# Normalising attention heads in two PSUM steps, with all engines ordered over two periods

## The chip, the cores and the metric

The kernel runs on one core of one Trainium2 chip. The metric is the device time of one launch in microseconds (us), the median of several runs of the whole program; smaller is better. The core has five engines that run at the same time, each working through its own queue strictly in order: TensorE (PE in the profile; its weight loads are listed apart as PEld), VectorE (DVE), ScalarE (ACT), GpSimd (POOL) and SyncE (SP), which issues DMA transfers. An instruction whose input is not ready holds up everything queued behind it on its engine.

## The reference, cut to what matters

The reference is a two-layer diffusion backbone over 2048 image tokens and 256 context tokens (2304 together), model width 1024. Layer 0 mixes a differential attention of 8 heads with a gated short convolution; layer 1 has a neighbourhood attention and a Fourier mix. The change touches layer 0 only, above all its attention. Each head has two score maps over all 2304 keys:

```python
def diff_attend(q, k, v, lam):
    s = einsum('bqhmd,bkhmd->bhmqk', q, k) * (A_QK ** -0.5)
    p = softmax(s, axis=-1)
    a = p[:, :, 0] - lam * p[:, :, 1]
    return einsum('bhqk,bkhd->bqhd', a, v)

def diff_attention_post(o, subln, lam_init):
    return (rms_norm(o, subln) * (1.0 - lam_init)).reshape(B, N, BRANCH_W)

def rms_norm(x, g):                 # over the 64 values of a head
    y = x * rsqrt(mean(x * x) + EPS)
    return y * g

out_a = diff_attention_post(o, subln, lam_init) * silu(ga)
```

The kernel leaves the first map's exponentials undivided. With Z0 and Z1 the sums of the two maps it computes o' = (e0 + cf e1) v with cf = -lam Z0 / Z1, which is Z0 times the wanted o. So rms_norm(o) = o' / sqrt(mean o'^2 + EPS Z0^2). Before the change this is computed as o' (1/Z0) / sqrt(mean o'^2 (1/Z0)^2 + EPS).

## The kernel before, in words

The program runs in stages: the input projection of layer 0 (`in_proj0`, with the small attention over the context in its gate part), the attention of layer 0 (`attention0`), the output projection, the input projection of layer 1, the Fourier mix, the attention of layer 1 and the last output projection.

`attention0` handles 8 heads times 16 tiles of 128 queries. Two tiles form one period, j = 0 to 63. A tile needs, for each of two maps m and three blocks of 768 keys: `QK` (PE writes scores into one of two PSUM tiles `ps`, L1014) and `TR` (DVE copies them to SBUF and takes the block's extreme, L766). Then `LS` (DVE), `LX` and `EX` (ACT: exponentials of 2304 values with their sum Z, L1053), `RC` and `CF` (DVE: 1/Z and the factor cf), and the combination e0 + cf e1: the first 256 columns on DVE (`CD`, L1067), the rest in two halves on POOL, `PS` (scale, L1072) and `PA` (add, L1077), 128x1024 each. PE transposes the result (`T`, L1084), ACT copies it out (`E`, L1091), PE multiplies it with the values (`AV`, L1101) into the PSUM tile `po`, of which there is one. `MA` (ACT) and `MD` (DVE, L1122, once a period) add the two halves of `po` into `ob`, the output of a head pair for 512 queries.

A hand-made list, `ATT_ORDER`, gives each of these steps a time within the period, and every period repeats it 18602 units later. The steps of all periods are sorted by that time, and `pin` (L191) chains the instructions of each engine in that order, so that the list sets every engine's queue. The entries `F` pull in PE matmuls of the convolution's input projection (`cmm`, L697, "fills"), some 43 a period. When 24 of them are through, the steps that follow on the other engines are put into the queues a given number of units later (`run_late`): z = c u (ACT, DVE), the three taps (`middle` on POOL, L727; `sides` on DVE, L730), the gate (DVE, L743) and its use (`out` on POOL, L749).

A head pair's `ob` for 512 queries is complete in every second period of each odd head, four times in eight periods; 16 times in all. `normalise` (L769) then makes nine steps of it: `squares` (ACT), `means` (8 small matmuls into `pms`), `factors` (four DVE instructions and one power on POOL, L794), `scaled` (DVE, L797), `rows` (matmuls into `pf`) and `rows_out` (ACT), `spread` (matmuls into `pr`, and the load of the gate `ga`), `scale` (DVE, L816) and `gate` (DVE: times the weight `sublnc` and the gate, L819; then the store). `pms`, `pf` and `pr` use the same single PSUM tile as `po`, so they must fit between two periods' `AV`. The steps are queued at fixed distances behind `MD` (L1132, L1135): `squares` to `factors` behind the `MD` that completes `ob`, `rows` behind the next one, `spread` behind the one after. The last of the 16 is done outside the list, beside the output projection.

Of the kernel before, what the change touches and what calls it, by code (L numbers as in the profile page):

```python
# [9 lines left out]
F32 = mybir.dt.float32  # L10
# [7 lines left out]
P = 128  # L18
# [20 lines left out]
ATT_PERIOD = 18602  # L39
# [6 lines left out]
QK000:0 QK001:829 TR000:904 F0:1176 F1:1658 TR001:1939 QK002:2140 TR002:2975 LS00:4169 QK010:4502 QK011:5439  # L46
LX0:6231 TR010:6660 TR011:7695 QK012:7972 EX00:8335 TR012:8731 QK100:8881 F2:9446 QK101:9928 F3:10275
LS01:10517 TR100:10671 EX01:11337 TR101:11707 QK102:12342 F4:12689 TR102:12879 QK110:13607 RC0:13915 F5:13954
LS10:14073 CF0:14227 LX1:14277 F6:14436 TR110:14447 QK111:14918 PS00:15584 F7:16137 CD0:16824 EX10:17085
PS01:17230 TR111:17230 QK112:17555 F8:17902 TR112:18266 PA01:18470 F9:18949 LS11:19352 EX11:19556 PA00:20912  # L50
RC1:22613 CF1:22925 T00:23605 E00:24241 T01:24388 CD1:24855 T02:24983 E01:25033 PS11:25262 E02:25625
PS10:26501 T03:26921 PA10:27741 T04:27830 E03:29347 PA11:30183 T10:31773 E04:33079 E10:33455 T11:33867
T12:34303 E11:34503 E12:35095 T13:35721 T14:36986 AV0:39786 E13:40567 AV1:40646 E14:41159 AV2:44116 AV3:48056
AV4:48916 MA:50951 MD:52686
"""
ATT_ORDER = [((x.split(":")[0].rstrip("0123456789"), tuple(int(d) for d in x.split(":")[0].lstrip("ACDEFKLMPQRSTVX"))),
              int(x.split(":")[1])) for x in ATT_ORDER.split()]

# [86 lines left out]
class Backbone:  # L145
# [278 lines left out]
    def in_proj0(self, sil):  # L424
# [3 lines left out]
        with ExitStack() as es:  # L428
# [205 lines left out]
    def conv_units(self, es):  # L634
# [46 lines left out]
        for si, (j, ci) in enumerate(steps):  # L681
# [4 lines left out]
            for br in range(3):  # L686
# [30 lines left out]
                elif br == 1:  # L717
# [14 lines left out]
                    def edge(z=z, last=last):  # L732
                        if not last:
# [3 lines left out]
                           (1500, middle), (3000, lambda sides=sides: sides(0)), (4500, lambda sides=sides: sides(2)),  # L737
                           (4600, edge)]
                else:
# [12 lines left out]
                    yield [(400, gate), (1500, out)]  # L752
# [16 lines left out]
    def normalise(self, ep, pp, hp, o, zi, t0, n, tags=("sq", "fr", "fr"), bank="fin", order=False):  # L769
# [29 lines left out]
        def rows():  # L799
            pf = st["pf"] = pp.tile([P, 512], F32, tag=bank, name="pf")  # L800
            for j in range(nt):
                self.pin(nc.tensor.matmul(pf[0:2, j * P:j * P + P], f[:, 2 * j:2 * j + 2], self.ident,
                                          start=True, stop=True))

        def rows_out():
            fr = st["fr"] = ep.tile([P, n], F32, tag=tags[1], name="fr")[0:2]
            pin(nc.scalar.activation(fr, st["pf"][0:2, :n], AF.Copy))

        def spread():
            pr = st["pr"] = pp.tile([P, 512], F32, tag=bank, name="pr")  # L810
            self.pin(nc.tensor.matmul(pr[:, :n], self.sel2, st["fr"], start=True, stop=True))
            ga = st["ga"] = ep.tile([P, n], F32, tag=tags[2], name="ga")
            nc.sync.dma_start(ga, self.ga[hp * P:hp * P + P, t0:t0 + n])
# [8 lines left out]
        return squares, means, factors, scaled, rows, rows_out, spread, scale, gate  # L822

    @staticmethod
    def quarters(steps):

        def some(fs):
            def run():
                for f in fs:
                    f()  # L830
            return run
        return [some(steps[a:b]) for a, b in ((0, 1), (1, 4), (4, 6), (6, 9))]

    def ctx_attention(self, cp, pp):
# [5 lines left out]
        def head(h):  # L840
# [3 lines left out]
            def scores():  # L844
# [11 lines left out]
                for qt in range(2):  # L856
# [3 lines left out]
                    Z = cp.tile([P, 2], F32, tag="Z", name="cZ", bufs=2)  # L860
# [9 lines left out]
                    for m in range(2):  # L870
                        nc.scalar.activation(s[m], s[m], AF.Exp, bias=bias[:, m:m + 1], scale=-1.0,
                                             accum_out=Z[:, m:m + 1])
                    rz = zi[:, qt, hh, :]
                    nc.vector.reciprocal(rz, Z)
                    cf = cp.tile([P, 1], F32, tag="cf", name="ccf", bufs=2)
                    nc.vector.scalar_tensor_tensor(cf, rz[:, 1:2], Z[:, 0:1], self.lam, ALU.mult, ALU.mult)
# [43 lines left out]
    def attention0(self, ws, xs, ys, ps_t, ps_o):  # L920
# [7 lines left out]
        CD = 256  # L928
        w = (T - CD) // NPC
        with ExitStack() as es:  # L930
# [42 lines left out]
            now, late, last, todo = [0], [], [], []  # L973
# [5 lines left out]
            def tile_of(j, n):  # L979
                i = 2 * j + n  # L980
                if i not in its:
# [4 lines left out]
                    it.Z = ep.tile([P, 2], F32, tag="Z", name="Z", bufs=4)  # L986
# [63 lines left out]
            def EX(j, n, m):  # L1050
                it = tile_of(j, n)
                bias = it.bias[:, 1:2] if m else it.low
                pin(nc.scalar.activation(it.s[m], it.s[m], AF.Exp, bias=bias, scale=-1.0, accum_out=it.Z[:, m:m + 1]))  # L1053


            def RC(j, n):
                it = tile_of(j, n)
                pin(nc.vector.reciprocal(it.rz, it.Z))

            def CF(j, n):  # L1060
                it = tile_of(j, n)
                pin(nc.vector.scalar_tensor_tensor(it.cf, it.rz[:, 1:2], it.Z[:, 0:1], self.lam, ALU.mult, ALU.mult))
# [51 lines left out]
            def MD(j):  # L1114
# [9 lines left out]
                if hh == 1 and it.qt % 4 == 3:  # L1124
# [4 lines left out]
                    else:  # L1129
                        st = self.normalise(ep, fin, hp, obs.pop((hp, c)), zis.pop((hp, c)), c * 512, 512, order=True)  # L1130
# [4 lines left out]
                for x in [x for x in todo if x[0] == j]:  # L1135
                    todo.remove(x)
                    run_late(x[1], x[2])
# [47 lines left out]
            for i, (op, t) in enumerate(ATT_ORDER):  # L1185
                for j in range(64):
                    trace.append((t + j * ATT_PERIOD, j, i, op))
            for t, j, _, (name, args) in sorted(trace, key=lambda x: x[:3]):
# [3 lines left out]
                OPS[name](j, *args)  # L1192
# [836 lines left out]
```

## Time and profile before

| what | value |
|---|---|
| median of 3 runs | 3454.68 us (3454.09 to 3458.59) |
| the profiled execution: its own time | 3461.83 us |
| its span in the trace | 3459.9 us |
| mean granted TensorE clock | 0.977 of 2.4 GHz |
| busy, share of the span | PE 95%, PEld 76%, DVE 53%, ACT 46%, POOL 42% |
| attention of layer 0: first and last `MD` (L1122) | 691.5 and 2062.5 us |

The profile is of one execution. A busy PE is not PE at its peak: matmuls are pipelined and their ends are modelled, and the granted clock can be half. "Idle before, releaser" gives the time an engine stood still just before an instruction and what ended the wait. The share of busy time over the whole program is a mean of very different stages; in the attention all five engines work, and a wait on any of them can hold up the others. A window row gives from:to, its length, then the busy time (and number of instructions) of PE, PEld, DVE, ACT and POOL in this order, the granted TensorE clock as a share of 2.4 GHz, the mean busy share of the DMA engines and the GB/s they moved.

### The profile page before, as it was taken

Reading aid. Unit: us, or ns where it says so; the run is one execution under the profiler, and the core shown is the slowest. Engines: PE = TensorE matmul, PEld = TensorE weight load, DVE = VectorE, ACT = ScalarE, POOL = GpSimd, SP = SyncE. Lnnn points to the kernel's source line nnn. Section 1 sums busy time; section 2 is a strip of 40 time slices with the busy share of each in tenths; the row PEclk is TensorE's granted clock in tenths of the full one; section 3 lists DMA queues with packets and bytes.
Section 4 is the critical chain, followed back from the end, with each engine's and each line's share of the span. In section 5 each row is a group of like instructions: output and inputs, shape, how many; then the busy total and the mean of one; then the engine's idle time right before and its main releaser. Section 6 shows DMA issues by size and latency. Waiting matters only on the chain. (4 is left out here: it accounts for less than half of the span.)

```text
span 3459.9 us, 54092 instructions
## 1 busy us (share of the span) xinstructions
PE 3281.5 (95%) x20386; PEld 2628.9 (76%) x20386; DVE 1839.9 (53%) x4155; ACT 1589.3 (46%) x2521; POOL 1452.6 (42%) x1185
## 2 busy tenths in 40 slices
PE   7999999899889999998999879999999999989999
PEld 6877777777667777777777557898888887778887
DVE  4343322578877777787777855331121014656743
ACT  4211242477667676776677543331111123556501
POOL 3133200388667777786777744310022001433400
PEclk9999999999999999999999899999999999999999
DMA  7366643523242333232322224453223257955143
GB/s 248 134 212 221 195 127 99 179 95 103 90 130 86 111 110 114 80 124 86 119 99 94 66 64 149 169 170 103 91 90 113 73 151 198 221 143 141 50 146 116
DMA packets 305318, 442.08 MB, mean 128 GB/s; under 512 B 54837, under 2 KB 212001, under 8 KB 292258
## 3 DMA queue, kind: packets, MB, share of 16 engines
q1 hardware_dynamic: 305058, 438.64, 40.2%
q8 instruction: 161, 2.64, 0.3%
q14 instruction: 99, 0.81, 0.1%
HBM read 307.59 MB, written 131.43 MB: 127 GB/s over the span
## 5 line engine op out<-in xcount | busy, mean ns | idle before, releaser
L766 DVE CUSTOM_DVE_ANT_0 s<-ps,zero 128x768 f32<-128x768 f32 x768 | 717.7, 953 | 237.3 <-PE ps L1014 234.7
L386 PE MATMUL mm<-hx,wh 128*128 128x512 f32 (+1 forms) x2784 | 830.9, 382 | 0.0
L1077 POOL TENSOR_TENSOR s<-s 128x1024 f32<-128x1024 f32 x256 | 614.0, 2413 | 9.4
L386 PEld LDWEIGHTS mm<-hx,wh 128*128 128x128 f32 x2784 | 505.6, 188 | 122.5 <-issue 18.0
L1014 PE MATMUL ps<-kst,qst 128*128 128x512 f32 (+1 forms) x1536 | 461.4, 383 | 82.2 <-DVE mx L766 75.2
L386 PE MATMUL mm<-hx,wl 128*128 128x512 f32 (+1 forms) x1392 | 528.5, 380 | 0.0
L1091 ACT ACTIVATE aT<-pt 128x512 f32<-128x512 f32 (+1 forms) x640 | 332.7, 550 | 197.6 <-PE pt L1084 193.2
L1072 POOL TENSOR_SCALAR s<-s,cf 128x1024 f32<-128x1024 f32 x256 | 309.2, 1218 | 261.6 <-ACT low L1048 108.1
L1014 PEld LDWEIGHTS ps<-kst,qst 128*128 128x128 f32 x1536 | 240.4, 196 | 185.4 <-DVE mx L766 107.3
L1084 PE MATMUL pt<-sm,s 128*128 128x128 f32 x2304 | 361.0, 281 | 18.8 <-POOL s L1077 12.7
L697 PE MATMUL cmm<-cx,wh 128*128 128x256 f32 x1728 | 356.7, 291 | 5.1 <-DMA cx<-hx 2.8
L1084 PEld LDWEIGHTS pt<-sm,s 128*128 128x128 f32 x2304 | 273.8, 144 | 65.1 <-ACT aT L1091 18.6
L1053 ACT ACTIVATE s<-s,bias 128x2304 f32<-128x2304 f32 x128 | 283.9, 2218 | 83.6 <-DVE bias L1042 82.9
L1101 PE MATMUL po<-aT,vt 128*64 128x256 f32 x2304 | 303.4, 400 | 0.0
L386 PEld LDWEIGHTS mm<-hx,wl 128*128 128x128 f32 x1392 | 261.3, 188 | 53.4
L697 PEld LDWEIGHTS cmm<-cx,wh 128*128 128x128 f32 x1728 | 279.7, 193 | 18.9 <-DVE cg L743 2.8
L1053 ACT ACTIVATE s<-s,low 128x2304 f32<-128x2304 f32 x128 | 283.4, 2214 | 0.0
L697 PE MATMUL cmm<-cx,wl 128*128 128x256 f32 x864 | 248.3, 287 | 0.0
L1101 PEld LDWEIGHTS po<-aT,vt 128*64 128x64 f32 x2304 | 153.0, 141 | 99.7 <-issue 40.7
L1905 POOL TENSOR_SCALAR s<-s,rz 128x832 f32<-128x832 f32 (+1 forms) x128 | 123.2, 963 | 203.7 <-DVE rz L1904 145.5
L1246 PE MATMUL y<-wh,mh 128*128 128x512 f32 x544 | 183.2, 415 | 9.9 <-DVE mh L1324 9.1
L1246 PE MATMUL y<-wl,mh 128*128 128x512 f32 x544 | 174.3, 399 | 0.0
(265 smaller groups left out, 4734.9 us busy)
## 6 DMA issues: line engine op xcount, KB each, us to landing
cx<-hx SPq DMA_DIRECT2D x72, 1024.0 KB
hx<-hx SPq DMA_DIRECT2D x18, 1024.0 KB
kst<-k SPq DMA_DIRECT2D x192, 96.0 KB
k<-k SPq DMA_DIRECT2D x32, 576.0 KB
xt<-in_x_dram SPq DMA_DIRECT2D x32, 512.0 KB
wm<-in_w_mod_dram SPq DMA_DIRECT2D x64, 256.0 KB
qst<-q SPq DMA_DIRECT2D x256, 64.0 KB
ws<-in_w_in_even_dram SPq DMA_DIRECT2D x27, 512.0 KB
```

Of the source, the lines that this page charges most:

```text
L386: mm = self.nc.tensor.matmul(ps[:, :n], p[:, kc], y, start=first, stop=last)
L697: yield nc.tensor.matmul(ps, w[p][:, kc, :], x[q][:, kc, :], start=i == 0, stop=i == 23)
L766: return self.nc.vector.tensor_tensor_reduce(dst, ps, self.zero.to_broadcast([P, n]), -QS, BIGGEST, ALU.add, ALU.min, mx)
L1014: pin(nc.tensor.matmul(ps[:, k0:k1], q[:, qc:qc + P], k[:, k0:k1], start=True, stop=True))
L1053: pin(nc.scalar.activation(it.s[m], it.s[m], AF.Exp, bias=bias, scale=-1.0, accum_out=it.Z[:, m:m + 1]))
L1072: pin(nc.gpsimd.tensor_scalar(x, x, it.cf, 1.0, ALU.mult, ALU.mult))
L1077: pin(nc.gpsimd.tensor_tensor(it.s[0][:, cs], it.s[0][:, cs], it.s[1][:, cs], ALU.add))
L1084: pin(nc.tensor.transpose(pt[:, i * P:i * P + P], it.s[0][:, k0:k0 + P], self.ident))
L1091: pin(nc.scalar.activation(it.aT[g][:, 0:k, n * P:n * P + P], it.pt.pop(g)[:, 0:k * P].rearrange("p (k q) -> p k q", q=P), AF.Copy))
L1101: pin(nc.tensor.matmul(it.po[c:c + 64, 0:256], vts[it.h][:, kt, :], it.aT[g][:, i, :], start=kt < 2, stop=kt >= 16, tile_position=(0, c)))
L1246: self.pin(self.nc.tensor.matmul(ps[hf] if isinstance(ps, list) else ps[:, cs], x, w[kc][:, cs], start=kc == 0 and i == 0, stop=kc == 7 an ...
L1905: nc.gpsimd.tensor_scalar(s[:, :w], s[:, :w], rz, 1.0, ALU.mult, ALU.mult).ins]
```

## The change

`ATT_ORDER` now covers two periods (four tiles), 36858 units, and holds the steps of `normalise` as entries of its own: `NS`, `NM`, `NF`, `NP`, `NB`, `NR`, `NO`, `NG`. The sum Z0 stays as it is (EX of map 0 writes it into `zi`), only Z1 is inverted. `normalise` loses three DVE instructions of `factors`, `scaled` and the pair `rows`/`rows_out`; it gains a small ACT square of sqrt(EPS) Z0 and `widen`, an ACT copy that repeats each factor 64 times, so that four plain transposes (`spread`) bring it into place. The gate moves from DVE to POOL, and the weight `sublnc` is applied on DVE where the gate is made, in the input projection. `CD` takes 320 columns and `PS` and `PA` 992. Three delays behind the fills grow.

```diff
-ATT_PERIOD = 18602
+ATT_PERIOD = 36858
-LX0:6231 TR010:6660 TR011:7695 QK012:7972 EX00:8335 TR012:8731 QK100:8881 F2:9446 QK101:9928 F3:10275
+MD1:67609 NS:69409 NM:72012 NF:74013 NP:75213 NB:79870 NR:84297 NO:85497 NG:87768
...
                     nc.scalar.activation(g[:, :n], ps, AF.Silu)
+                    if dst is self.ga:
+                        nc.vector.tensor_scalar(g[:, :n], g[:, :n], self.sublnc, None, ALU.mult)
...
-                           (1500, middle), (3000, lambda sides=sides: sides(0)), (4500, lambda sides=sides: sides(2)),
-                           (4600, edge)]
+                           (2500, middle), (4500, lambda sides=sides: sides(0)), (6000, lambda sides=sides: sides(2)),
+                           (6100, edge)]
-                    yield [(400, gate), (1500, out)]
+                    yield [(400, gate), (3000, out)]
...
-            st["sq"] = ep.tile([P, n], F32, tag=tags[0], name="sq")
-            pin(nc.scalar.activation(st["sq"], o, AF.Square))
+            sq = st["sq"] = ep.tile([P, n], F32, tag=tags[0], name="sq")
+            pin(nc.scalar.activation(sq, o, AF.Square))
+            pin(nc.scalar.activation(f, zi.rearrange("p t h m -> p (t h) m")[:, :, 0], AF.Square, scale=math.sqrt(EPS)))
...
-            zf = st["zf"] = ep.tile([P, 8], F32, tag="zf", name="zf")[:, :2 * nt]
-            pin(nc.vector.tensor_copy(zf, zi.rearrange("p t h m -> p (t h) m")[:, :, 0]))
-            pin(nc.vector.tensor_tensor(f, st["pms"][:, :2 * nt], zf, ALU.mult))
-            pin(nc.vector.tensor_tensor(f, f, zf, ALU.mult))
-            pin(nc.vector.tensor_scalar(f, f, EPS, None, ALU.add))
+            pin(nc.vector.tensor_tensor(f, st["pms"][:, :2 * nt], f, ALU.add))
+            ga = st["ga"] = ep.tile([P, n], F32, tag=tags[1], name="ga")
+            nc.sync.dma_start(ga, self.ga[hp * P:hp * P + P, t0:t0 + n])
+
+        def roots():
             pin(nc.gpsimd.tensor_tensor(f, f, self.mhalf.to_broadcast([P, 2 * nt]), ALU.pow))
-        def scaled():
-            pin(nc.vector.tensor_tensor(f, f, st["zf"], ALU.mult))
-        def rows():
...
+        def widen():
+            fb = st["fb"] = ep.tile([P, n], F32, tag=tags[2], name="fb")
+            pin(nc.scalar.activation(fb.rearrange("p (f c) -> p f c", c=64), f.unsqueeze(2).to_broadcast([P, 2 * nt, 64]),
+                                     AF.Copy))
         def spread():
             pr = st["pr"] = pp.tile([P, 512], F32, tag=bank, name="pr")
-            self.pin(nc.tensor.matmul(pr[:, :n], self.sel2, st["fr"], start=True, stop=True))
+            for j in range(nt):
+                self.pin(nc.tensor.matmul(pr[:, j * P:j * P + P], st["fb"][:, j * P:j * P + P], self.ident, start=True,
+                                          stop=True))
         def gate():
-            pin(nc.vector.scalar_tensor_tensor(o, st["ga"], self.sublnc, o, ALU.mult, ALU.mult))
+            pin(nc.gpsimd.tensor_tensor(o, o, st["ga"], ALU.mult))
...
-        CD = 256
+        CD = 320
...
-                pin(nc.scalar.activation(it.s[m], it.s[m], AF.Exp, bias=bias, scale=-1.0, accum_out=it.Z[:, m:m + 1]))
+                pin(nc.scalar.activation(it.s[m], it.s[m], AF.Exp, bias=bias, scale=-1.0,
+                                         accum_out=it.Z if m else it.rz[:, 0:1]))
-                pin(nc.vector.reciprocal(it.rz, it.Z))
+                pin(nc.vector.reciprocal(it.rz[:, 1:2], it.Z))
...
-                        todo.extend((j + d // 100, t, st[i]) for i, (d, t) in enumerate((
-                            (0, 50), (0, 900), (0, 1300), (0, 6000), (100, 200), (100, 600), (200, 200), (200, 600),
-                            (200, 5000))))
+                        norms[j // 2] = self.normalise(ep, fin, hp, obs.pop((hp, c)), zis.pop((hp, c)), c * 512, 512,
+                                                       order=True)
...
+                if name[0] == "N":
+                    if j in norms:
+                        norms[j]["SMFPBROG".index(name[1])]()
+                else:
+                    OPS[name](2 * j + args[0], *args[1:])
```

The lines of the changed kernel stand some 4 to 13 further down than before: `PS` is L1078, `PA` L1083, the transposes L1090, `QK` L1019, `AV` L1107, `means` L797, `factors` L802, the power L807, the gate on POOL L824. What an instruction waits for stands in brackets, by the engine whose signal it needs.

The first place is GpSimd's queue at a completed `ob` in the first odd head. `s<-s,cf` is `PS`, `s<-s` is `PA`, `f<-f,mhalf` is the power, `y<-y,cg` belongs to the convolution. Before:

```order
L1072 TENSOR_SCALAR s<-s,cf 128x1024 [waits DVE_49,PE_49,Activation_49]
L794 TENSOR_TENSOR f<-f,mhalf 128x8 [waits DVE_49]
L1072 TENSOR_SCALAR s<-s,cf 128x1024
L1077 TENSOR_TENSOR s<-s 128x1024 [waits Pool_49]
L710 MEMSET z 128x2
L714 MEMSET z 128x1
L1077 TENSOR_TENSOR s<-s 128x1024
```

And after the change, from the add ahead of the power to the gate (`ob<-ob,ga`):

```order
L1083 TENSOR_TENSOR s<-s 128x992 [waits Pool_49]
L807 TENSOR_TENSOR f<-f,mhalf 128x8 [waits DMAHW6_49,DMAHW2_49,DVE_49]
L1083 TENSOR_TENSOR s<-s 128x992 [waits Pool_49]
L1078 TENSOR_SCALAR s<-s,cf 128x992 [waits DVE_49,PE_49,Activation_49]
L1078 TENSOR_SCALAR s<-s,cf 128x992
L1083 TENSOR_TENSOR s<-s 128x992 [waits Pool_49]
L724 COPY z<-ez 128x2
L726 MEMSET z 128x1
L1083 TENSOR_TENSOR s<-s 128x992
L824 TENSOR_TENSOR ob<-ob,ga 128x512 [waits DMAHW4_49,DMAHW2_49,DMAHW5_49,DMAHW0_49,DVE_49]
L1078 TENSOR_SCALAR s<-s,cf 128x992 [waits DVE_49,PE_49,Activation_49]
```

The power moved from between the two scalings of a tile to between its two adds, half a tile later; the gate is new on this queue, at the end of a tile's adds.

The second place is TensorE's queue at `means` in the second odd head (`pt` are the transposes, `ps` the scores, `cmm` the fills). Before:

```order
L1084 MATMUL pt<-sm,s 128x128 [waits Pool_49]
L1084 MATMUL pt<-sm,s 128x128
L697 MATMUL cmm<-cx,wl 128x256
L784 MATMUL pms<-sm,sq 128x2 [waits Activation_49]
L784 MATMUL pms<-sm,sq 128x2 x3
L1084 MATMUL pt<-sm,s 128x128 [waits Activation_49]
L1084 MATMUL pt<-sm,s 128x128 x3
```

And after:

```order
L1090 MATMUL pt<-sm,s 128x128 [waits Pool_49]
L1090 MATMUL pt<-sm,s 128x128
L1019 MATMUL ps<-kst,qst 128x512 [waits DVE_49]
L1019 MATMUL ps<-kst,qst 128x256
L797 MATMUL pms<-sm,sq 128x2 x4
L1090 MATMUL pt<-sm,s 128x128 [waits Activation_49]
```

Before, `means` waits for the squares on ScalarE; after, it stands late enough that an earlier wait of TensorE already covers them, and it has no wait of its own.

The third place is TensorE's queue behind that, where the first score blocks of the next tile stand. Before:

```order
L1014 MATMUL ps<-kst,qst 128x512 [waits DMAHW4_49,DMAHW3_49,DVE_49]
L1014 MATMUL ps<-kst,qst 128x256
L697 MATMUL cmm<-cx,wh 128x256
L697 MATMUL cmm<-cx,wl 128x256
L697 MATMUL cmm<-cx,wh 128x256 x2
L697 MATMUL cmm<-cx,wl 128x256
L1014 MATMUL ps<-kst,qst 128x512 [waits DVE_49]
```

And after:

```order
L1019 MATMUL ps<-kst,qst 128x512 [waits DMAHW5_49,DMAHW4_49,DVE_49]
L1019 MATMUL ps<-kst,qst 128x256
L1019 MATMUL ps<-kst,qst 128x512 [waits DVE_49]
L1019 MATMUL ps<-kst,qst 128x256
L1090 MATMUL pt<-sm,s 128x128 [waits Activation_49]
L1090 MATMUL pt<-sm,s 128x128
L1107 MATMUL po<-aT,vt 64x256 [waits DVE_49]
```

The fills that stood between the first two score blocks are gone; the two blocks stand back to back, and the first `AV` (`po`) behind them waits for DVE, which must have read `pms` out of the shared PSUM tile.

## Rows read from the trace of the kernel before

**Rows 1.** Stretches between `MD` starts: length, busy time by engine, clock, DMA share, GB/s.
```profile
691.50:865.60 174.10, 168.90 (x1254) 136.45 (x1253) 139.57 (x351) 133.32 (x194) 140.20 (x94) 1.00 0.30 99
865.60:1037.70 172.10, 149.91 (x1037) 116.75 (x1036) 137.46 (x307) 112.33 (x170) 116.80 (x78) 0.95 0.34 109
1037.70:1225.30 187.60, 176.02 (x1264) 140.15 (x1263) 140.43 (x350) 134.67 (x196) 139.65 (x95) 0.97 0.31 101
1225.30:1389.40 164.10, 150.09 (x1038) 117.22 (x1036) 127.34 (x304) 111.87 (x171) 116.99 (x76) 0.96 0.34 107
1389.40:1565.60 176.20, 170.68 (x1265) 136.96 (x1264) 138.90 (x352) 134.46 (x195) 140.60 (x96) 1.00 0.32 102
1565.60:1732.60 167.00, 150.61 (x1034) 117.08 (x1033) 129.37 (x303) 112.22 (x170) 117.64 (x78) 0.95 0.35 111
1732.60:1915.20 182.60, 173.20 (x1264) 138.37 (x1263) 141.54 (x351) 134.33 (x196) 137.98 (x94) 0.98 0.27 86
1915.20:2053.70 138.50, 113.85 (x626) 76.28 (x625) 100.98 (x201) 74.86 (x112) 96.83 (x67) 0.88 0.16 52
```

**Rows 2.** The power alone (L794) in two of the same stretches, GpSimd's busy time.
```profile
865.60:1037.70 172.10, 7.32 (x4) 0.95 0.34 109
...
1915.20:2053.70 138.50, 5.47 (x3) 0.88 0.16 52
```

**Rows 3.** One `MD` on DVE's timeline: start, duration, engine, line, operation.
```profile
865.56 0.43 DVE L1122 TENSOR_TENSOR ob<-po,ft 64x256 f32<-64x256 f32 x1
```

**Rows 4.** Waits in 640 to 1820 us: total, times, longest.
```profile
POOL s L1072 <- ACT low L1048: 90.8, 43, 5.1
PEld ps L1014 <- DVE mx L766: 80.7, 96, 4.3
...
POOL f L794 <- DVE f L793: 43.1, 12, 4.7
...
POOL y L749 <- DVE cg L743: 34.4, 16, 5.2
...
POOL y L727 <- DVE z L736: 25.9, 7, 10.0
```

**Rows 5.** GpSimd's timeline around one power; in brackets the idle time before.
```profile
1364.73 1.13 POOL L1072 TENSOR_SCALAR s<-s,cf 128x1024 f32<-128x1024 f32 x1 [0.21 <-ACT aT L1091]
1369.63 1.83 POOL L794 TENSOR_TENSOR f<-f,mhalf 128x8 f32<-128x8 f32 x1 [3.77 <-DVE f L793]
```

**Rows 6.** TensorE's timeline: the `means` matmuls ahead of that power.
```profile
1367.93 1.00 PE L784 MATMUL pms<-sm,sq 128*128 128x2 f32 x8
```

**Rows 7.** DVE's timeline: its wait for those matmuls.
```profile
1368.97 0.17 DVE L791 TENSOR_TENSOR f<-pms,zf 128x8 f32<-128x8 f32 x1 [1.12 <-PE pms L784]
```

**Rows 8.** Groups of instructions in 640 to 1820 us: busy, mean ns, idle before.
```profile
L1077 POOL TENSOR_TENSOR s<-s 128x1024 f32<-128x1024 f32 x218 | 523.0, 2414 | 8.2
...
L1072 POOL TENSOR_SCALAR s<-s,cf 128x1024 f32<-128x1024 f32 x218 | 261.8, 1211 | 216.8 <-ACT low L1048 90.8 <-DMA cx<-hx 55.5 <-DVE cf L1062 39.3
...
L819 DVE SCALAR_TENSOR_TENSOR ob<-ga,sublnc,ob 128x512 f32<-128x512 f32 x12 | 24.7, 2056 | 1.9 <-DMA ga<-ga 1.9
```

**Rows 9.** The gate on DVE (L819), whole program: duration ns min/median/max, first and last start.
```profile
L819 DVE SCALAR_TENSOR_TENSOR ob<-ga,sublnc,ob x16: 741/1942/2886, 914.4 to 2092.3; 128x512 f32<-128x512 f32 x16
```

**Rows 10.** The chain that ended last, around the last period: start, us, what.
```profile
2039.51 0.44 PE pt L1084 x4
...
2063.13 3.11 DMA ga<-ga
2066.34 0.76 DVE ob L819
2067.11 2.51 DMA mixa<-ob
...
2070.67 5.37 DMA xt<-in_ctx_dram
```

**Rows 11.** A window of the gate projections, where `ga` is made; columns as in Rows 1.
```profile
560.00:600.00 40.00, 40.00 (x188) 29.20 (x188) 4.15 (x15) 6.43 (x12) 1.11 (x2) 1.00 0.23 75
```

More of the change, by code (lines that the diff above doesn't have):

```diff
@@ L51 @@
[L51 to L54, printed above, removed]
-"""
-ATT_ORDER = [((x.split(":")[0].rstrip("0123456789"), tuple(int(d) for d in x.split(":")[0].lstrip("ACDEFKLMPQRSTVX"))),
-              int(x.split(":")[1])) for x in ATT_ORDER.split()]
+QK0000:0 QK0001:349 TR0000:1266 TR0001:3756 QK0002:3791 TR0002:4792 QK0010:5725 LS000:5986 TR0010:6919 F00:6946
@@ new lines @@
+QK0011:7446 QK0012:8231 TR0011:8375 F01:8580 LX00:9023 EX000:9323 TR0012:9411 QK0100:9734 F02:10083 TR0100:10447
+LS001:11483 QK0101:11532 QK0102:11881 F03:12230 TR0101:12472 EX001:12701 F04:12730 TR0102:13508 QK0110:13666
+F05:14015 F06:14515 TR0110:14544 QK0111:15015 RC00:15580 CF00:15788 F07:15800 TR0111:16008 QK0112:16299
+PS001:16553 LS010:17044 LX01:17248 F08:17520 QK1000:18020 EX010:18090 CD00:18454 PS000:18962 TR0112:18962
+TR1000:19998 PA000:20163 QK1001:20602 F09:20951 LS011:21034 QK1002:21451 EX011:21468 F10:21800 TR1001:22038
@@ new lines @@
+F11:22300 PA001:22529 F12:22800 TR1002:23074 T000:23299 T001:23735 E000:23935 RC01:24110 QK1010:24171
+LS100:24268 CF01:24422 QK1011:24520 LX10:24527 E001:24777 CD01:24895 EX100:25369 PS011:26404 TR1010:26404
+T002:27314 TR1011:27440 PS010:27604 QK1012:27750 T003:28099 E002:28159 TR1012:28476 QK1100:28535 E003:28751
+PA010:28805 T004:28884 F13:29102 LS101:29562 F14:29602 TR1100:29716 EX101:29766 QK1101:30102 F15:30451
+QK1102:30951 PA011:31172 TR1101:31172 F16:31300 F17:31800 E004:32176 RC10:32226 QK1110:32299 CF10:32434
@@ new lines @@
+T010:32648 TR1102:32654 T011:33084 E010:33382 F18:33520 PS100:33538 TR1110:33690 QK1111:34020 T012:34369
+LS110:34726 PS101:34739 QK1112:34805 TR1111:34880 LX11:34930 E011:35180 E012:35772 TR1112:35916 T013:35922
+F19:36358 EX110:36364 LS111:37002 PA100:37039 T014:37556 AV00:37869 AV01:38729 E013:38774 E014:39366 AV02:39589
+EX111:39742 CD10:40106 PA101:40614 AV03:41093 AV04:41953 MA0:42633 RC11:42686 T100:42932 CF11:42998 CD11:43268
+T101:43368 E100:43623 PS111:43776 E101:44215 T102:44652 MD0:44812 PS110:44977 E102:45288 T103:45937 PA110:46178
@@ L60, in dft_tables @@
+T104:46373 PA111:48544 E103:48590 E104:49182 T110:50088 E110:51968 T111:52221 E111:52857 T112:53506 T113:53942
+E112:54356 T114:55227 AV10:55540 AV11:56400 E113:57358 E114:57950 AV12:61822 AV13:62682 AV14:63542 MA1:64637
+MD1:67609 NS:69409 NM:72012 NF:74013 NP:75213 NB:79870 NR:84297 NO:85497 NG:87768
+"""
+ATT_ORDER = [((x.rstrip("0123456789"), tuple(int(d) for d in x[len(x.rstrip("0123456789")):])), int(t))
+             for x, t in (y.split(":") for y in ATT_ORDER.split())]
 def dft_tables():
@@ L767, in reduce_scores, with normalise @@
                                               ALU.min, mx)
-    def normalise(self, ep, pp, hp, o, zi, t0, n, tags=("sq", "fr", "fr"), bank="fin", order=False):
+    def normalise(self, ep, pp, hp, o, zi, t0, n, tags=("sq", "ga", "sq"), bank="fin", order=False):
         nc = self.nc
@@ L818, in gate @@
         def gate():
-            pin(nc.vector.scalar_tensor_tensor(o, st["ga"], self.sublnc, o, ALU.mult, ALU.mult))
+            pin(nc.gpsimd.tensor_tensor(o, o, st["ga"], ALU.mult))
             self.stored = nc.sync.dma_start(self.mixa[0][t0 // 512][hp * P:hp * P + P], o)
-        return squares, means, factors, scaled, rows, rows_out, spread, scale, gate
+        return squares, means, factors, roots, widen, spread, scale, gate
     @staticmethod
@@ L831, in some @@
             return run
-        return [some(steps[a:b]) for a, b in ((0, 1), (1, 4), (4, 6), (6, 9))]
+        return [some(steps[a:b]) for a, b in ((0, 1), (1, 4), (4, 7), (7, 8))]
     def ctx_attention(self, cp, pp):
@@ L859, in scores @@
                     bias = cp.tile([P, 2], F32, tag="bias", name="cbias", bufs=2)
-                    Z = cp.tile([P, 2], F32, tag="Z", name="cZ", bufs=2)
+                    Z = cp.tile([P, 1], F32, tag="Z", name="cZ", bufs=2)
+                    rz = zi[:, qt, hh, :]
                     ps = pp.tile([P, 512], F32, tag="tp", name="cps")
@@ L972, in attention0 @@
             obs, zis = {}, {}
-            now, late, last, todo = [0], [], [], []
+            now, late, last, norms = [0], [], [], {}
             def run_late(d, *steps):
@@ L985, in tile_of @@
                     it.mx = ep.tile([P, 2, 3], F32, tag="mx", name="mx", bufs=4)
-                    it.Z = ep.tile([P, 2], F32, tag="Z", name="Z", bufs=4)
+                    it.Z = ep.tile([P, 1], F32, tag="Z", name="Z", bufs=4)
                     it.bias = ep.tile([P, 2], F32, tag="bias", name="bias", bufs=4)
@@ L1185, in attention0 @@
             for i, (op, t) in enumerate(ATT_ORDER):
-                for j in range(64):
+                for j in range(32):
                     trace.append((t + j * ATT_PERIOD, j, i, op))
```

27 lines of the change are left out of this document (4 added, 23 removed).

## The prediction

> **What bounds the kernel now.** The change works in the attention of layer 0, so I cut that stage by itself. I took the starts of `MD`, which comes once in a period [rows 3], and cut windows at those starts where the heads change character [rows 1]. The power of `normalise` shows which is which: four in the second stretch (and as many in the fourth and sixth), three in the last, none in the others [rows 2]. The reader should see two kinds of stretch. The four plain ones hold 9 periods each and last 174.1 + 187.6 + 176.2 + 182.6 = 720.5 us, 20.01 us a period. The three others with fills hold 7 periods each and last 172.1 + 164.1 + 167.0 = 503.2 us, 23.96 us a period, though each period has the same matmuls and four extra short groups. The surplus is 3.95 x 21 = 83 us for 12 normalisations, 6.9 us each.
>
> In the plain stretches PE is busy (168.90 + 176.02 + 170.68 + 173.20) / 36 = 19.13 of 20.01 us: TensorE is the bound there, and a better order can win little. In the normalising stretches it is idle for 23.96 - 21.46 = 2.50 us a period instead of 0.88, and its busy time has grown by 2.3 us with the granted clock at 0.95 to 0.96 instead of 0.97 to 1.00 [rows 1]: part of the time stands at the lower of the two levels, 1.2 GHz, after the idle gaps.
>
> The waits say where it begins. GpSimd stood 43.1 us in 12 waits, 3.6 us each, ahead of the power, for DVE [rows 4]. One such place in time order [rows 5]: `PS` at 1364.73, then 3.77 us idle, then the power for 1.83 us, and only then the tile's next `PS`. GpSimd waits for the small DVE work, DVE for the `means` matmuls [rows 7], and these for the squares; they take 1.00 us [rows 6]. All this sits at the head of GpSimd's queue between the two halves of a tile, so the tile's adds, its transposes and its `AV` come 3.6 + 1.8 = 5.4 us late. That is most of the 6.9.
>
> **The change part by part.** All sums are against the profiled execution, 3461.83 us (3459.9 span and 1.9 around it); the median of the three runs is 7.15 us lower, so the gain is finally taken from 3454.68.
>
> Normalisation, removed: 12 x 6.9 = 83 us, and in the last stretch, where 5 periods take 138.5 us against 5 x 20.01 = 100.1, 3 of the same price, 21 us, of the 38 us surplus; the rest belongs to the split of the output weights, which stays. Gross 104 us. The wait goes because in the new order the power stands half a tile later, between the two adds, and `means` has no wait of its own on TensorE.
>
> Normalisation, what stays or comes: on TensorE the `means` matmuls, 1.00 us [rows 6], and four transposes, 0.44 us [rows 10], in place of three groups; TensorE is nearly full, so 1.44 us count. The power keeps its 1.83 us on GpSimd, which in plain stretches is busy (140.20 + 139.65 + 140.60 + 137.98) / 36 = 15.51 of 20.01 us; it delays an add, but 4.5 us are free in a period, so between 0 and 1.83 us count, and I take 1.0, the middle, because the queue is in order and part of its slack lies elsewhere. The gate on GpSimd is not in the trace. From below it is 0, if hidden where `PS` waits for ScalarE's exponentials, 90.8 / 43 = 2.1 us a time [rows 4], ahead of which it is queued; from above half of a two-input add over 1024 columns, 2414 / 2 = 1.21 us [rows 8]. I take 0, since 1.21 is less than 2.1. On DVE 2.06 us a time go with it [rows 8], no gain counted since DVE is not the bound. The new ACT work (a square of 8 columns and a 512-column copy) is covered by ScalarE's idle time, (133.32 + 134.67 + 134.46 + 134.33) / 36 = 14.9 us busy in a plain period [rows 1]; uncovered, it would cost less than 1 us of the 6.9 once per normalisation, at most 15 us. So 1.44 + 1.0 = 2.4 us return, 15 x 2.4 = 37, and the net is 104 - 37 = 67 us; bounds 0 (the wait turns up elsewhere in full) and 104.
>
> A sentence of the Trainium skill speaks against moving the gate: GPSIMD Engine Reference, section 4.1 Engine selection, puts an elementwise operation of two inputs on VectorE because GpSimd is about twice as slow at it. Here the same gate on DVE took 0.74 us at best but 2.06 us in this stage [rows 8, 9]; twice the best would be an estimate of 1.5 us on GpSimd, and if it all counted the sum would be 15 x 1.5 = 22 us worse. Since 1.21 us is the bound from rows, the rule holds against DVE alone and not against DVE beside a busy GpSimd.
>
> Order of the plain periods. The bounds come from the stretches themselves: the best runs at 174.1 / 9 = 19.34 us, the worst at 187.6 / 9 = 20.84. For some 48 periods without a normalisation that is a gain of 32 or a loss of 40 us. The convolution's later entries aim at GpSimd's 34.4 and 25.9 us of waits for DVE [rows 4], 60 us in 54 periods (218 `PS` at four a period [rows 8]); if a quarter of it was on the path, 15 us return. I take +15. Moving 64 columns of each tile from POOL to DVE takes 2 x (2414 + 1211) x 32/1024 = 227 ns from GpSimd per tile and adds less to DVE: nothing counted, since neither is the bound; with GpSimd's cover gone it would be worth 0.45 us a period.
>
> End of the stage. Behind the last period the chain runs through the load of `ga` 3.11, the gate 0.76, the store 2.51 and a load held up behind it in SP's queue, 5.37 us [rows 10]. The list now ends the third chunk's normalisation within the last period and loads `ga` already at `factors`. Of the first three, 6.4 us, I count 6; bounds 0 and 10. SP's queue loses that late store and gains no transfer.
>
> The weight on the gate, 20 more DVE instructions in the input projection: TensorE is busy 40.0 of 40 us there and DVE 4.15 [rows 11], so nothing; without that cover some 0.7 us each, 14 us.
>
> Sum: 67 + 15 + 6 = 88, rounded down to 87 us: 3374.8 against the profiled time, and 3454.68 - 87 = 3368 us as median. Its own range: from 3454.7 - (104 + 32 + 10) = 3309 to 3454.7 - 30 = 3425.
>
> **The rivals.** *The wait only moves.* Then `f` is late again: GpSimd waits ahead of the power for DVE, or at the gate for `scale`, or `AV`, which now waits for DVE to have read `pms`, takes over. For it: everything still passes through the one PSUM tile, and each queue is still in order. Against: the power has a whole add ahead of it, 2.4 us. The normalising stretches stay near 24 us a period; only 15 + 6 us come, 3434 us.
>
> *Nothing comes of it.* TensorE is 95% busy over the program, and if its lost time in the normalising stretches came from the low clock for other reasons, the gain would be within a few microseconds, 3450 to 3458. Against it stands the surplus of 6.9 us exactly where the power is.
>
> *Slower: the score tiles.* In the new order the first two score blocks of a tile stand back to back on TensorE without fills between them, with only two PSUM tiles, so the third must wait for DVE's `TR` in a queue with more columns of `CD`. Before, TensorE waited 80.7 us for these reads in those 54 periods, 1.5 us a period [rows 4]. If that doubles, 64 x 1.5 = 96 us are added and the result is 3368 + 96 = 3464. It decides from 87 / 64 = 1.36 us a period on. For it: every period is touched, and idle TensorE falls to 1.2 GHz. Against: DVE loses the gate's 2.06 us at each normalisation [rows 8], and before the change the blocks filled both tiles too.
>
> **How the numbers follow.** The forecast 0.60, the moved wait 0.17, nothing 0.08, the score tiles 0.15. About 0.2% of 3454, 7 us, is what a measurement can tell from no change. Faster by more than that: 0.60 + 0.17 = 0.77; within it 0.08; slower 0.15. For the range I start at 3305, beyond which only the sum of all upper bounds lies (0.04), and go up through the moved wait to 3455, which leaves out half of "nothing" and all of the slower case, 0.04 + 0.15.
>
> **What would show it.** Right: stretches cut at `MD` as above are alike, near 19.7 us plain and 22 us or less with the power; GpSimd's wait ahead of the power falls from 3.6 to below 1 us; the granted clock there is back at 0.98 or more; the waits of `y` on DVE shrink; the store of the third chunk lies before the last `MD`. Wrong: GpSimd or `AV` waiting more than 3 us for DVE at each normalisation; plain stretches above 21 us with TensorE waiting for `mx`; or a loss outside the attention, above all in the gate projections.

## The result, and the profile after

| | median | runs |
|---|---|---|
| before | 3454.69 us | 3454.09 to 3458.59 |
| after | 3334.15 us | 3330.37 to 3336.15 |

The ratio is 0.9647 (95% interval 0.9631 to 0.9664): 120 us or 3.5% faster. The forecast was 87 us, 3368 us, with a range of 3305 to 3455. The profiled execution after the change has a span of 3328.6 us and a mean granted clock of 0.990.

The same cuts at `MD` starts (L1128 now) give the stretches after. Since two periods are no longer alike, each stretch here holds an even number of periods, eight, and the last five. Columns as in [rows 1]; the second, fourth, sixth and last stretch hold the normalisations.

```profile
697.20:848.60 151.40, 146.41 (x1113) 120.85 (x1114) 123.98 (x310) 119.32 (x174) 121.00 (x85) 1.00 0.33 112
848.60:1010.50 161.90, 155.07 (x1182) 131.22 (x1182) 135.60 (x322) 126.83 (x198) 133.38 (x91) 0.98 0.39 128
1010.50:1162.60 152.10, 146.38 (x1109) 120.41 (x1107) 125.14 (x313) 118.56 (x174) 121.86 (x86) 1.00 0.34 112
1162.60:1323.20 160.60, 154.47 (x1176) 129.70 (x1177) 135.51 (x325) 127.09 (x197) 132.41 (x91) 0.99 0.39 129
1323.20:1478.70 155.50, 147.02 (x1119) 121.74 (x1118) 126.74 (x309) 118.64 (x174) 122.08 (x84) 1.00 0.29 95
1478.70:1646.70 168.00, 154.99 (x1173) 130.21 (x1171) 141.32 (x325) 127.01 (x198) 133.67 (x92) 0.98 0.36 120
1646.70:1809.50 162.80, 150.00 (x1114) 124.27 (x1115) 134.89 (x313) 119.73 (x174) 120.74 (x85) 0.98 0.26 87
1809.50:1930.40 120.90, 97.18 (x593) 70.76 (x592) 91.94 (x192) 73.64 (x113) 93.27 (x66) 0.93 0.18 61
```

Plain periods take (151.4 + 152.1 + 155.5 + 162.8) / 32 = 19.43 us instead of 20.01, normalising ones (161.9 + 160.6 + 168.0) / 24 = 20.44 instead of 23.96. The surplus of a normalisation, which comes in every second period, is 2.0 us instead of 6.9, and its clock is back at 0.98 to 0.99.

GpSimd's timeline around one power of the new order answers [rows 5]: the power follows a tile's first add without a wait, and the gate (L824) a tile's last add.

```profile
1290.33 2.33 POOL L1083 TENSOR_TENSOR s<-s 128x992 f32<-128x992 f32 x1
1292.60 1.69 POOL L807 TENSOR_TENSOR f<-f,mhalf 128x8 f32<-128x8 f32 x1
1294.23 2.58 POOL L1083 TENSOR_TENSOR s<-s 128x992 f32<-128x992 f32 x1
1298.43 2.44 POOL L1078 TENSOR_SCALAR s<-s,cf 128x992 f32<-128x992 f32 x2 [1.63 <-PE po L1107]
1300.81 0.20 POOL L724 COPY z<-ez 128x2 f32<-128x2 f32 x1
1300.96 4.62 POOL L1083 TENSOR_TENSOR s<-s 128x992 f32<-128x992 f32 x2
1305.54 1.30 POOL L824 TENSOR_TENSOR ob<-ob,ga 128x512 f32<-128x512 f32 x1
```

The waits of 630 to 1820 us after the change answer to [rows 4] (total, times, longest): the one ahead of the power fell from 43.1 to 7.8 us, GpSimd's waits for `z` and `cg` from 25.9 and 34.4 to 11.7 and 8.7, TensorE's for the score copies from 80.7 to 62.1.

```profile
PEld ps L1019 <- DVE mx L778: 62.1, 68, 4.3
...
POOL y L739 <- DVE z L748: 11.7, 6, 3.3
...
POOL y L761 <- DVE cg L755: 8.7, 6, 5.1
POOL f L807 <- DVE f L802: 7.8, 8, 2.7
```

The chain behind the last period (answering [rows 10]) stays on TensorE: between the last `AV` and the next stage there is no load of `ga`, no store and no load behind it.

```profile
1944.48 4.04 PE po L1107 x36
1948.51 2.99 PE y L1250 x12
1951.50 0.86 PE pg L1240 x2
1952.36 0.79 PE pms L797 x8
1953.14 1.50 PE y L1250 x6
```

### The profile page after: what moved, and what is told of

Read it like the earlier page. It is cut to its first block, busy times and chain, and to the rows that moved or that the text cites. A ratio compares the mean times of both kernels' runs of the same rounds, so it can differ in the third digit from the quotient of the medians.

```text
span 3328.6 us, 53884 instructions
## 1 busy us (share of the span) xinstructions
PE 3190.3 (96%) x20346; PEld 2609.0 (78%) x20346; DVE 1818.0 (55%) x4075; ACT 1588.2 (48%) x2541; POOL 1447.5 (43%) x1205
## 5 line engine op out<-in xcount | busy, mean ns | idle before, releaser
L1083 POOL TENSOR_TENSOR s<-s 128x992 f32<-128x992 f32 x256 | 595.5, 2340 | 7.2
L1019 PE MATMUL ps<-kst,qst 128*128 128x512 f32 (+1 forms) x1536 | 428.0, 367 | 74.3 <-DVE mx L778 65.8
L1078 POOL TENSOR_SCALAR s<-s,cf 128x992 f32<-128x992 f32 x256 | 301.2, 1187 | 238.4 <-DVE cf L1068 106.0
L1019 PEld LDWEIGHTS ps<-kst,qst 128*128 128x128 f32 x1536 | 236.2, 192 | 141.7 <-DVE mx L778 87.3
L1090 PE MATMUL pt<-sm,s 128*128 128x128 f32 x2304 | 340.2, 277 | 6.0 <-ACT aT L1097 5.4
L1090 PEld LDWEIGHTS pt<-sm,s 128*128 128x128 f32 x2304 | 270.8, 143 | 42.2 <-ACT aT L1097 13.2
L1107 PE MATMUL po<-aT,vt 128*64 128x256 f32 x2304 | 277.3, 385 | 0.8 <-DVE f L802 0.8
L1107 PEld LDWEIGHTS po<-aT,vt 128*64 128x64 f32 x2304 | 153.9, 136 | 93.6 <-issue 26.1
L1250 PE MATMUL y<-wh,mx 128*128 128x512 f32 x544 | 173.3, 397 | 0.0
```

What stands on the lines that cost most here:

```text
L1019: pin(nc.tensor.matmul(ps[:, k0:k1], q[:, qc:qc + P], k[:, k0:k1], start=True, stop=True))
L1078: pin(nc.gpsimd.tensor_scalar(x, x, it.cf, 1.0, ALU.mult, ALU.mult))
L1083: pin(nc.gpsimd.tensor_tensor(it.s[0][:, cs], it.s[0][:, cs], it.s[1][:, cs], ALU.add))
L1090: pin(nc.tensor.transpose(pt[:, i * P:i * P + P], it.s[0][:, k0:k0 + P], self.ident))
L1107: pin(nc.tensor.matmul(it.po[c:c + 64, 0:256], vts[it.h][:, kt, :], it.aT[g][:, i, :], start=kt < 2, stop=kt >= 16, tile_position=(0, c)))
L1250: self.pin(self.nc.tensor.matmul(ps[hf] if isinstance(ps, list) else ps[:, cs], x, w[kc][:, cs], start=kc == 0 and i == 0, stop=kc == 7 an ...
```

## The experiments

Times are medians; 3454 us is before, 3334 after. Each ratio is to the kernel before, run beside it, with its 95% interval. That interval reaches about 6 us either way, so two runs must lie some 8 us apart to be told from each other.

**1. Old kernel, only the power moved** between the two adds, and `scaled`, which uses it, 2500 units later.

```diff
+        def roots():
             pin(nc.gpsimd.tensor_tensor(f, f, self.mhalf.to_broadcast([P, 2 * nt]), ALU.pow))
-   (0, 50), (0, 900), (0, 1300), (0, 6000), (100, 200), ...
+   (0, 50), (0, 900), (0, 1300), (0, 5400), (0, 8500), (100, 200), ...
```

> The kernel before, with one step moved: the power on GpSimd stands half a tile later, between the two adds of a tile, and the DVE step that uses it (scaled) 2500 units later; algorithm, three PSUM groups and main order as before. Theory A (GpSimd's wait ahead of the power, 3.6 us in 15 normalisations, and the tile it holds up are the main loss): 40 to 65 us of the 120 come back, about 3400. Theory B (the shorter algorithm with two PSUM groups and the gate off DVE brings it): less than 15 us, 3440 or more.

Measured 3430.67, ratio 0.9935 (0.9916 to 0.9953): 24 us, between the two theories. GpSimd's wait ahead of the power did go, from 43.1 to 7.0 us, but TensorE's wait for the score copies stayed (80.7 before), and DVE still waits for `pr` (14.6 before too). Waits of 640 to 1820 us:

```profile
PEld ps L1016 <- DVE mx L766: 82.3, 89, 4.7
...
DVE ob L818 <- PE pr L813: 14.6, 11, 1.6
...
POOL f L796 <- DVE f L793: 7.0, 7, 2.9
```

So the wait that I had called most of the surplus was worth 1.6 us a normalisation, not 5.4: of the 3.0 us by which each wait shrank, about half came back as time.

**2. New kernel, `means`, `factors` and power early again.**

```diff
- NM:72012 NF:74013 NP:75213
+ NM:70100 NF:71000 NP:71500
```

> The changed kernel, with means, factors and power 1900 to 3700 units earlier, so that the power stands between the two scalings of a tile again and waits there for DVE; everything else as changed. Theory A: the stall is back, 3 to 5 us for 15 normalisations, 45 to 75 us slower than the changed kernel, about 3390. Theory B: within 10 us of the changed kernel, 3334 to 3344.

Measured 3352.00 (ratio to before 0.9703, 0.9677 to 0.9729): 18 us slower than after, about a seventh of the 120. GpSimd waited 17.0 us ahead of the power in 640 to 1820 us, not the 43.1 of before, so the old stall came back only in part. The run moves three steps together and does not tell them apart.

**3. Old main order, new normalisation.** The old list written out twice, the eight new entries set in.

```diff
-ATT_PERIOD = 36858
+ATT_PERIOD = 37204
+ NS:72288 NM:74400 NF:75600 NP:76700 NB:81000 NR:91000 NO:92200 NG:97700
```

> The changed kernel with the main steps in the order of before (its list written out twice, period 2 x 18602) and the new normalise steps set into it at places like those of the new list (power between the adds, means before the next AV). It tells the new main order from the new normalisation. If the normalisation alone accounts for my 67 us plus the end of the stage: 3454 - 85 = about 3370, 35 us above the changed kernel. If the main order brings more than I gave it (15): 3385 to 3400. If it brings nothing: 3340 or less.

Measured 3391.99 (0.9821, 0.9803 to 0.9839): 62 us below before, 58 above after; the new delays and `CD` are in it too. The 58 us that are missing are far more than the 15 that I gave the main order, but they need not be the order alone: the eight places were set by hand in the old list, and GpSimd still waits there ahead of the power (640 to 1820 us; 43.1 before, 7.8 after):

```profile
POOL f L808 <- DVE f L803: 23.2, 12, 3.7
```

**4. New kernel, old delays behind the fills.**

```diff
-  (2500, middle), ... (4500, ... sides(0)), (6000, ... sides(2)), (6100, edge)   [(400, gate), (3000, out)]
+  (1500, middle), ... (3000, ... sides(0)), (4500, ... sides(2)), (4600, edge)   [(400, gate), (1500, out)]
```

> The changed kernel with the delays of the convolution's steps behind the fills as before (1500, 3000, 4500, 4600 and 1500 units). If the later delays are what makes the plain periods shorter, GpSimd's waits for DVE ahead of y come back and the time rises by 15 to 30 us, to about 3355; if the plain periods gain by the main order, it stays within 5 us of 3334.

Measured 3353.17 (0.9708, 0.9691 to 0.9725): the delays are worth 19 us in the new kernel. (The change lengthens five of them, not three.)

**5 and 6. Both kernels without the 15 normalisations.**

```diff
-                        st = self.normalise(ep, fin, hp, obs.pop((hp, c)), zis.pop((hp, c)), c * 512, 512, order=True)
...
+                            self.stored = nc.sync.dma_start(self.mixa[0][c][hp * P:hp * P + P], ob)
+                        run_late(5000, put)
```

That is the old kernel's edit; the new kernel's is the same at its own call of `normalise`. `put` holds the store alone: both kernels leave the normalisation of these 15 pieces out and store `ob` as it is.

> The kernel before without the 15 normalisations inside the attention: ob is stored as it is (that part of the computation is left out; the 16th stays). It gives the whole price of them before the change. If they are the surplus of the odd heads (7.0 us each, 12 measured, 3 more in the last stretch): 3454 - 15 x 7 - a few us at the end of the stage = 3335 to 3350, and plain and odd stretches alike. If half of the surplus belongs to the odd heads for other reasons: 3390 to 3400.

> The changed kernel without the same 15 normalisations (left out in the same way). It gives what they still cost after the change and what the main order gains by itself, against the run of the old order without them. Surplus 2.0 us each in the changed kernel: 3334 - 30 = 3300 to 3310. The gap to the old order without them is the main order, the delays and CD together: 20 us if I sized the plain periods rightly, 35 us or more if the new order is worth that in every period.

Measured 3348.15 (0.9690, 0.9670 to 0.9709) and 3320.96 (0.9611, 0.9597 to 0.9626). The price of 15 normalisations was 3453 - 3348 = 105 us, 7.0 each, and is 3334 - 3321 = 13 us, 0.9 each, which is little more than two runs can tell apart. The rest of the change, without any normalisation to disturb it, is 3348 - 3321 = 27 us. These two numbers, 92 and 27, make the 120.

The traces say more than the medians. In run 5 the stretches of the odd heads, cut at `MD` as above, are still the slower ones, though nothing is normalised in them; here are the first two:

```profile
858.20:1023.70 165.50, 153.41 (x1114) 123.28 (x1113) 136.00 (x315) 122.11 (x186) 123.61 (x83) 0.97 0.37 119
1186.40:1354.70 168.30, 154.13 (x1114) 123.18 (x1113) 138.32 (x317) 121.84 (x185) 125.58 (x83) 0.97 0.36 117
```

The three odd stretches run at 493.0 / 24 = 20.54 us a period and the four plain ones at 630.2 / 32 = 19.69. So 1.7 of the 7 us of surplus per normalisation remain without any. One thing that the odd stretches have besides is the split of the convolution's weights on VectorE (`wl`, L659): 12 subtractions, 11.2 us, in the first stretch shown and none in the plain one behind it. No run shows that it is the cause. In run 6 the remainder is 1.0 us, half of the 2.0 seen after the change, so that its other half agrees with the price of 0.9.

Leaving the work out also shortens the passage from the last `AV` to the first transpose of the next stage, from 31.0 to 17.5 us; after the change it is 15.5.

**7. Run 1 and the gate on GpSimd besides.** The weight `sublnc` moves into the input projection with it, and the gate stands 500 units later.

```diff
-  pin(nc.vector.scalar_tensor_tensor(o, st["ga"], self.sublnc, o, ALU.mult, ALU.mult))
+  pin(nc.gpsimd.tensor_tensor(o, o, st["ga"], ALU.mult))
```

> The kernel before with the power moved as in the first run, and besides with the gate on GpSimd behind a tile's adds (the weight applied where the gate is made). Theory A2 (what is left of the surplus is VectorE's queue: some 5 us of normalise instructions and its waits delay the score copies, and TensorE waits for them): 2.06 us less on VectorE each time, 15 to 30 us below that run's 3431, so 3400 to 3415. Theory P (VectorE has room, the gate does not count): within 8 us of 3431; by a page's rule on two-input operations GpSimd would even be slower, 3435 to 3450.

Measured 3435.76 (0.9944, 0.9928 to 0.9961), 5 us above run 1, which is within the noise. Theory A2 falls as far as the gate goes: VectorE's 2 us were not the price.

**8. New kernel, gate on VectorE.**

```diff
-  pin(nc.gpsimd.tensor_tensor(o, o, st["ga"], ALU.mult))
+  pin(nc.vector.tensor_tensor(o, o, st["ga"], ALU.mult))
```

> The changed kernel with the gate (one two-input multiplication, 128x512) back on VectorE at the same place of the list. Theory A2: VectorE's queue is longer by 0.7 to 2 us at 15 places, 10 to 30 us slower than 3334. Theory P: within 6 us of 3334, or faster by up to 10 us, since GpSimd loses 1.3 us.

Measured 3336.19 (0.9657, 0.9642 to 0.9671), the same as after within the noise.

**9. Old kernel, all nine steps spaced out.**

```diff
- (0, 50), (0, 900), (0, 1300), (0, 5400), (0, 8500), (100, 200), (100, 600), (200, 200), (200, 600), (200, 5000)
+ (0, 1000), (0, 3100), (0, 4300), (0, 5400), (0, 8500), (100, 1500), (100, 2900), (200, 1500), (200, 2900), (200, 6500)
```

> The kernel before with all nine steps of normalise spaced out (power between the adds as in the first run, squares 1000, means 3100, factors 4300 units behind MD instead of 50, 900 and 1300; rows, rows_out, spread and scale 1500 and 2900 behind the later MDs instead of 200 and 600). Algorithm as before: three PSUM groups, gate and all small steps on VectorE. Theory S (the price of a normalisation, 106 us in all, is a chain of short waits on three engines behind MD; the distances make it): another 25 to 45 us below the first run's 3431, so 3385 to 3405, as far as the new normalise gets in the old order. Theory G (three PSUM groups and the longer VectorE work make it): 3420 to 3435.

Measured 3437.64 (0.9949, 0.9931 to 0.9967): nothing beyond run 1 (7 us above it, within the noise). Theory S falls for these distances, the only ones tried, and the trace shows what came in between. TensorE's wait for the score copies shrank to 61.0 us and DVE's for `pr` went, but two others came: TensorE waits for `scale` of the chunk before (L818) ahead of `means`, and GpSimd again ahead of the power. First the waits of 640 to 1820 us, then two rows of TensorE's and GpSimd's timelines:

```profile
PEld ps L1016 <- DVE mx L766: 61.0, 70, 5.5
...
POOL f L796 <- DVE f L793: 41.8, 12, 8.0
...
PE pms L784 <- DVE ob L818: 14.1, 9, 5.1
```
```profile
1264.43 1.87 PE L784 MATMUL pms<-sm,sq 128*128 128x2 f32 x8 [5.15 <-DVE ob L818]
```
```profile
1268.92 1.68 POOL L796 TENSOR_TENSOR f<-f,mhalf 128x8 f32<-128x8 f32 x1 [8.04 <-DVE f L793]
```

This points to the single PSUM tile: `means` cannot write it before `scale` has read it. With three groups, `spread` and `scale` of one chunk and `means` and `factors` of the next fall into the same gap between `MD` and the next `AV`, in this order, so spacing one pushes the other; `means` stands 200 units behind `scale` here, 300 before. With two groups over two periods each gap holds one, by the places in the list.

**10. Old kernel, new delays.** The edit of run 4 the other way round.

> The kernel before with the changed kernel's delays behind the fills (2500, 4500, 6000, 6100, 3000 units). In the changed kernel the old delays cost 19 us. If they are worth the same in the old order: 3435; if the normalisations' stalls cover them: 3447 to 3458.

Measured 3455.72, ratio 1.0006 (0.9993 to 1.0020): nothing. The delays' 19 us do not appear in the old kernel; whether its order or its normalisations cover them was not taken apart.

**11. New kernel, the 15th chunk's spread, scale and gate held back to the end of the attention.**

```diff
-                    if j in norms:
+                    if j == 30 and name[1] in "ROG":
+                        held.append(norms[j]["SMFPBROG".index(name[1])])
+                    elif j in norms:
```

> The changed kernel, with spread, scale and gate of the last chunk normalised within the attention (the 15th) held back until all steps of the attention are queued, as it was before the change. If its early end is what shortened the passage from the attention to the output projection (31 us to 16 between the last AV and the first transpose of the next stage): 8 to 15 us slower than 3334. If the passage is shorter for another reason: within 4 us.

Measured 3349.64 (0.9694, 0.9677 to 0.9711): 15.5 us slower, and the chain at the end is the old one again:

```profile
1956.58 0.70 DVE ob L821
...
1957.34 1.27 POOL ob L824
1958.63 2.04 DMA mixa<-ob
...
1961.69 7.60 DMA xt<-in_ctx_dram
...
1969.36 2.37 POOL xt L1286
```

**12. New kernel, still longer delays** (3500, 5500, 7000, 7100 and 4500).

> The changed kernel with the delays behind the fills lengthened once more (3500, 5500, 7000, 7100 and 4500 units). GpSimd still waits some 30 us for DVE ahead of y in the attention. If these waits are on the path: 3322 to 3330; if what is left of them is covered: within 5 us of 3334; a step that lands later holds up its neighbour: slower by up to 10 us.

Measured 3340.79 (0.9667, 0.9649 to 0.9684), 7 us slower than after, at the edge of what two runs can tell apart. GpSimd's waits for `z` and `cg` shrank further, to 5.0 and 0.8 us (640 to 1820 us), and brought nothing. No version that computes everything beat the changed kernel.

## Why the prediction was right, and where its steps were off

*Direction and place: right.* The gain lies where the stretches of [rows 1] put it. The forecast's gross price of the normalisations, 104 us, and the 105 of run 5 agree in part by luck. The forecast took the whole surplus of the odd and the last stretches for the normalisations. Without them the three odd stretches, eight periods each, shrink by 71 us (563.7 to 493.0) and the last one by 14, where 83 and 21 were forecast; what run 5 has besides is the passage behind the attention (13.5 us) and some 10 us in the plain stretches, neither of which stood in the 104. The price after the change was forecast at 2.4 us each by returned work and is 0.9 by run 6, though one term of it was too small: the four transposes of `spread` run as eight matmuls (`pr`, x8), 0.89 us at 1937.73 in the chain after the change, not 0.44. The net of 67 is 92, of which 15 belong to the end of the stage, so 77 answer to the 67.

*The mechanism of that term: too narrow.* The step "the wait goes because the power stands half a tile later" failed as the cause. It put wait and power, 5.4 us, on the path in full; moving the power alone brought 24 us, 1.6 each. The wait ahead of it was one link of a chain, squares, `means`, `factors`, power, `scaled`, `rows`, `spread`, `scale`, on four engines and one PSUM tile. In run 1 that link went and TensorE's waits for the score copies stayed; in run 9 waits came up at other links, on TensorE ahead of `means` and on GpSimd ahead of the power. Run 1 landed at 3431, near the 3434 us of my rival "the wait only moves", but by luck: that sum held 15 and 6 us of other terms, and no wait of GpSimd or `AV` took the place of the one that went. The whole gain came only with the shorter algorithm in its own places (62 us with the old order, early end and new delays included) and with its fit to the new main order (the other 58).

*Order of the plain periods: mis-sized.* I had +15, from a quarter of GpSimd's waits of 60 us, and found 27 without any normalisation: inside the bounds of -40 to +32, but nearly twice the size. Little of it lies in the plain stretches themselves, which run at 19.69 us a period in run 5 and 19.47 in run 6; the odd ones go from 20.54 to 19.97. With the normalisations in place the delays alone are 19 us in the new kernel (run 4) and 0 in the old one (run 10): the terms are not additive, as the sum took them to be.

*End of the stage: mis-sized.* 6 us forecast, 15.5 in run 11. The rows had it: behind the store stood the load of 5.37 us, which I left out as not belonging to the chunk though it was queued behind it, and behind that an add of 2.37 us on GpSimd, as run 11 shows again.

*The edits costed at nothing.* The gate on either engine makes no difference clear of noise (runs 7 and 8, 5 and 2 us). The weight in the input projection costs nothing to be seen: the first score matmul of the attention starts at 633.6 us instead of 637.1. `CD` and the ScalarE copy `widen` were not run by themselves.

*The slower rival* did not happen: TensorE's wait for the score copies fell from 80.7 to 62.1 us in these windows, though their blocks stand back to back.

*Still open:* which of the pieces (the third PSUM group, `scaled` on VectorE, the ScalarE copy of two rows, the new delays, `CD`) carries the step from run 1 to run 3, 39 us with some 12 at the end of the stage; they were not taken apart. That the number of uses of the PSUM tile decides is argued from run 9 and the list, and no run changes it alone.

## What to carry to other kernels

Price a recurring disturbance by comparing stretches with and without it, and confirm it by leaving it out, stretch by stretch and not only in the total. Here the totals agreed, 104 and 105 us, while a quarter of the surplus stayed in its stretches and another place made up for it. The longest single wait inside the disturbance explained less than a quarter of its price. A chain of short steps across in-order engines and one shared buffer need not be mended at one link; see which uses fall into the same gap of the buffer. Gains of an order and of the delays tuned with it need not add up, so test an edit in the order it is meant for.

## What the runs showed of the hardware

A VectorE multiplication of 128x8 elements took 1353 ns on average in the kernel before (`f<-f,zf`, L797) and 156 ns in run 9, where only the places of the steps had changed. The first copy of `normalise` went the other way, 199 ns before and 1284 ns in run 1. The traces show the neighbour. In the kernel before, 11 of the 16 multiplications `f<-f,zf` of L797 took more than 1 us; each of them began while one of GpSimd's adds (`s<-s`, L1077) ran and ended within 0.03 us of that add's end. None of the other 5 did. In run 1, 10 of the 12 slow copies began beside the add (L1079 there) and ended within 0.1 us of its end, the other two beside a scaling. The ten gates on VectorE (L819) that began beside an add in the kernel before ended 0.54 to 0.55 us behind it; that mean of 2.06 us [rows 8] is mostly waiting of this kind, for the fastest took 0.74 us. One pair from the kernel before, GpSimd's two adds from 1372.66 to 1377.79 us and the multiplication from 1376.38 to 1377.82:

```profile
1372.66 5.13 POOL L1077 TENSOR_TENSOR s<-s 128x1024 f32<-128x1024 f32 x2
```
```profile
1376.38 1.44 DVE L797 TENSOR_TENSOR f<-f,zf 128x8 f32<-128x8 f32 x1
```

The means, before and in run 9:

```profile
L797 DVE TENSOR_TENSOR f<-f,zf 128x8 f32<-128x8 f32 x12 | 16.2, 1353 | 0.0
```
```profile
L799 DVE TENSOR_TENSOR f<-f,zf 128x8 f32<-128x8 f32 x12 | 1.9, 156 | 0.0
```

The two-input multiplication of 128x512 takes 1.30 us on GpSimd here, near the 1.21 us taken from half an add of 1024 columns [rows 8]. The Trainium skill's rule on such operations (GPSIMD Engine Reference, section 4.1 Engine selection) asks for VectorE, with GpSimd about twice as slow. The trace of run 8 agrees with the factor: there the same multiplication took 0.69 us on VectorE, the median of 16. The time of the program does not follow it: runs 7 and 8 show no difference beyond 5 us, within the noise.
